# A decoder trunk on one core: attention's output projection in seven block products for its first column pair too, the first heads' sums at attention's end, and the recurrence's functions taken by kind

## The chip, the cores and the metric

The kernel runs on 1 core of a Trainium2 chip. The metric is device time of one execution in microseconds (us). The engines are TensorE (PE, matmuls; its weight loads are PEld), VectorE (DVE), ScalarE (ACT), GpSimd (POOL) and SyncE (SP), which here issues transfers.

## The reference

Two layers over 256 tokens of width 2048, in fp32. Layer 0 mixes with two recurrences (RG-LRU and HGRN2), layer 1 with attention; each is followed by an output projection and an MLP.

```python
# RG-LRU of layer 0
r = sigmoid(x @ w_a + b_a); i = sigmoid(x @ w_i + b_i)
log_a = -8 * r * softplus(-lam)
a = exp(log_a); u = sqrt(-expm1(2 * log_a)) * (i * x)      # then h_t = a_t h_(t-1) + u_t
...
# layer 1
qkv = (h @ w_qkv).reshape(bsz, seq, 3, 16, 128)
...
out = (num / den).reshape(bsz, seq, 2048)                   # three dilated windows merged by softmax
h = h + out @ w_o                                           # w_o: 2048 x 2048
h = h + square(relu(rms_norm(h) @ w1)) @ w2
```

## The kernel before

Every fp32 weight passes TensorE as two parts: `hi`, its rounding to fp32r, made by a cast on ScalarE, and `lo`, the rest, made by a subtraction on VectorE. The activations are split in the same way, in halves of one tile (`bufa`, `bufb`). A product of a 128x512 piece of weight with 128 tokens is three matmuls: hi by hi, hi of the weight with lo of the activation, and lo of the weight with hi of the activation. A weight unit is 1 MB (four pieces of 128x512 rows); for the 256 tokens it takes 24 matmuls. Raw, hi and lo have three buffers each, so units are loaded and split up to three ahead.

**Block products.** Most matrices are taken a column pair (2 x 512 columns) at a time in `blocks`, which computes a 2x2 block product in seven products for eight. Seven products are named `a, t1, t2, c, t3, d, t4`; each takes 12 matmuls. Four of them take sums of weight tiles (`s` and `t`, added on VectorE or by an accumulating transfer from GpSimd's queue), and `t1, t2, t3, c` take sums of activations, which lie in split form in `formx` or `formh`, one part for each of four pairs m. Each of the four pairs stands for two 128-row pieces of the first half of the rows; the rest of the rows goes through plain units `n` of 24 matmuls. The order of the products of a column pair is a row of `ORDERS`.

For w_o, the projection behind attention, the second column pair ran in `blocks` (through `second`), and the first ran plainly in `tokens`: two column blocks n of four units g. Its rows came in the order `PAIRED`, and each unit was split in two halves of 1024 columns. `mixed_forms(m)` made the sums of heads 2m and 2m+1, between w_o's units; only the second pair read them.

**Attention.** w_qkv is taken in `columns`, six blocks of eleven steps, with the values of the last eight heads last. Between steps run the parts of a head from `attend`: `turned` (transposes), `scores` (with the softmax: Exp on ScalarE, normalising of tile `as` by `ll`), `weights` (transposes of `as`, copied to `qk`), `mixed` (the value product, split into `bufb`). The value products of heads 8 to 15 (`mixes`) run at w_o's start: four after its first unit, four after its second, and then `handover` closes attention's pools.

**The recurrence.** `lru_scan` runs on lane e, in ticks between the matmuls of the input projection; `TICKS` says after which half of a unit a lane moves. Letters a and b are the lanes of HGRN2. `lut` keeps ScalarE's functions in program order, and a function of another table brings an ACT_TABLE_LOAD.

A scheduler orders the instructions of each engine from the program and its priorities; within the input projection the order is as written (`InOrder`). Names in the rows drop to the tile: `L261` is the matmul of `mm`, `L264` the transpose, and `L68` every operation of VectorE and ScalarE that goes through the recording helper.

Of the kernel before, what the change touches and what calls it, by code (L numbers as in the profile page):

```python
# [10 lines left out]
F32 = mybir.dt.float32  # L11
# [9 lines left out]
P = 128  # L21
# [20 lines left out]
def trunk_kernel(ctx, tc, head, x, xtok, xback, cols, tab, masks, pos, fin, w_in, w_gate, w_out, w_qkv, w_o, w1, w2, out):  # L42
# [63 lines left out]
    def plan(src, n):  # L106
        units.extend((src, i) for i in range(n))

    order_of = lambda src, i: ORDERS[0 if src is w1 and i not in (0, 64, ) else 2 if src is w2 and i == 120 else 1]

    def plan2(src, i):
        for what, u in order_of(src, i):
# [9 lines left out]
    for layer in range(2):  # L122
        if layer:
            for i in range(0, 48, 8):
                plan2(w_qkv, i)
            plan(w_o, 8)
            plan2(w_o, 8)
        for q in range(4):
            for src in (w1, w2):
                for n in range(0, 4, 2):  # L130
                    plan2(src, layer * 64 + q * 16 + 4 * n)
# [239 lines left out]
            V.scalar_tensor_tensor(r, t, 1.5, r, op0=OP.add, op1=OP.mult)  # L371

    def tokens(src, i0, mov, kgs=(0, 1, 2, 3), by_k=False, behind=(), then=()):
        ks = PAIRED if src is w_o else range(KB)
        ps = [pmm.tile([P, 512], F32, name="p") for _ in range(2)]
        for g in kgs:
            w = unit(src, i0 + g)
            opens, ends = g == kgs[0], g == kgs[-1]
            hi, lo = ([t[:, i * 512:i * 512 + 512] for i in range(4)] for t in (w.hi, w.lo))
            xs = lambda i, j, at=0: mov[:, ks[4 * g + i], at + j * P:at + j * P + P]  # L380
            if by_k:
                for i in range(4):
                    if ends and i == 1:
                        chain.extend(behind)
                    if src is w_in and not ends:
                        parts = [(j, *p) for p in ((0, hi[i]), (S, hi[i]), (0, lo[i])) for j in range(2)]
                    else:
                        parts = [(j, *p) for j in range(2) for p in ((0, hi[i]), (0, lo[i]), (S, hi[i]))]
                        if opens and not i:
                            parts.insert(1, parts.pop(3))  # L390
                    for n, (j, at_, w_) in enumerate(parts):
                        mm(ps[j], xs(i, j, at_), w_, start=opens and not i and at_ == 0 and w_ is hi[0],
                           stop=ends and i == 3 and not any(p[0] == j for p in parts[n + 1:]))
                    if i % 2 and ticks:
                        tick(ticks.pop(0))
            else:
                for j in range(2):
                    if ends and not j:
                        chain.extend(behind)
                    parts = [(i, *p) for i in range(4) for p in ((0, hi[i]), (S, hi[i]))]  # L400
                    parts += [(i, 0, lo[i]) for i in range(4)]
                    for n, (i, at_, w_) in enumerate(parts):
                        mm(ps[j], xs(i, j, at_), w_, start=opens and not n, stop=ends and n == 11)
                    if ticks:
                        tick(ticks.pop(0))
            turn_some(1)
            for f in steps.pop(0) if steps else ():
                f()
            for m in then[kgs.index(g)] if then else ():
                mixed_forms(m)  # L410
        return ps

    def tick(which):
# [281 lines left out]

    def lru_scan(gp):
        gr, gi = rooms[gp][:, :4], rooms[gp][:, 4:]
        for half in range(2):
            for m in range(2 * half, 2 * half + 2):
                b = 4 * gp + m  # L700
                V.tensor_tensor(xc[:, b], xc[:, b], gi[:, m], OP.mult)
                lut(gi[:, m], gr[:, m], AF.Tanh, scale=sp4[:, b:b + 1])
                lut(gr[:, m], gr[:, m], AF.Exp, scale=sp8[:, b:b + 1])
                V.tensor_scalar(gi[:, m], gi[:, m], -1.0, 1e-30, op0=OP.mult, op1=OP.max)
            yield
        for m in range(4):
            lut(gi[:, m], gi[:, m], AF.Sqrt)
        for half in range(2):
            for m in range(2 * half, 2 * half + 2):
                b = 4 * gp + m  # L710
                V.scalar_tensor_tensor(gi[:, m], gr[:, m], 1.0, gi[:, m], op0=OP.add, op1=OP.mult)
                V.tensor_tensor(xc[:, b], xc[:, b], gi[:, m], OP.mult)
                V.tensor_tensor_scan(xc[:, b], gr[:, m], xc[:, b], 0.0, op0=OP.mult, op1=OP.add)
            yield
# [93 lines left out]
                part_forms(forms, k // 2, 1, slice(0, 4), z.rearrange("p i j (one c) -> p one (i j) c", one=1))  # L808
        turns.extend([-half if forms else 0, lambda half=half: work(half)] for half in range(2))

    def mixed_forms(m):
        z = pair.tile([P, 2, 2, P], F32, name="y1", bufs=2)
        b = bufb[:, 2 * m:2 * m + 2].bitcast(F32)
        V.tensor_tensor(z.rearrange("p i j c -> p i (j c)"), b[..., :S], b[..., S:], OP.add)
        a11, a21, a12, a22 = (z[:, i, j] for i in range(2) for j in range(2))
        combos(a22, a11, a21, a12, a11, a21, a12, a22)
        part_forms(formh, m, 1, slice(0, 4), z.rearrange("p i j (one c) -> p one (i j) c", one=1))

    def out_project(src, gname, kgs, behind=()):
        nrm = Norm()  # L820
        whole = any(src is w for w in (w_out, w_o, ))
        for n in range(2 if whole else 4):
            then = () if not whole else ((((), (), (0,), (1,)), ((2,), (3,), (), ())) if src is w_out else
                                         (((), (), (), (0, 1)), ((), (2,), (3,), ())))[n]
            add_res(tokens(src, 4 * n, bufb, kgs, src is w_o and not n, () if n else behind, then), n, nrm)
            to_features(n, gname, formx if n < 2 else None)
        if whole:
            second(0, 2, nrm, 1.0, -1.0, lambda n: to_features(n, gname, None), None, src)
        return nrm


    def blocks(src, i0, n0, mov, forms, events, final):
# [3 lines left out]
                "t1": lambda i: form(3, i), "t2": lambda i: form(0, i), "t3": lambda i: form(1, i),  # L836
                "c": lambda i: form(2, i)}
        alpha, delta, gamma = (pmm.tile([P, 512], F32, name="p") for _ in range(3))
        beta = psc.tile([P, 512], F32, name=("pd" if i0 % 16 else "pt") if src is w_qkv else "po" if n0 else "pd", bufs=1)
        bank = {"a": beta, "t1": alpha, "t2": beta, "c": alpha, "t3": beta, "d": gamma, "t4": beta}  # L840
        sums = {(0, 0): gamma, (0, 1): beta, (1, 0): alpha, (1, 1): delta}
        opened = []
# [102 lines left out]
        blocks(w1, i0, n0, bufa, formx, {"a": hold("y1", A.copy, 2), "t1": hold("y4", V.tensor_copy), "t2": hold("y2", A.copy),  # L945
                                             "t3": u3}, final)

    def second(i0, n0, nrm, r2, r2n, done, gains, src=w2):
        def to_x(bank, j, n, r, last):
            at = slice(n * 512, n * 512 + 512)  # L950
            with urgent():
# [24 lines left out]
        def u3(bank):  # L976
            to_x(bank, 1, n0 + 1, r2n, True)
            done(n0 + 1)

        blocks(src, i0, n0, bufb, formh,  # L980
               {"a": lambda b: to_x(b, 0, n0, r2, False), "t1": lambda b: to_x(b, 1, n0 + 1, r2, False),
                "t2": u2, "t3": u3, **ends},
               lambda n, j, b: to_x(b, j, n0 + n, r2, (n, j) != (1, 1)))
# [37 lines left out]
                second(layer * 64 + q * 16, n, ends, r2, r2n, done, gains if ends and not gname and not n else None)  # L1021
        return fing

    nrm = out_project(w_out, "nmlp0", (2, 3, 0, 1))
    nx1 = Norm()
    mlp(0, nrm, nx1, "nmix1")
    pairs.close()
# [63 lines left out]
    def attend(hd, z):  # L1091
# [12 lines left out]
        def scores():  # L1104
            with urgent():
# [10 lines left out]
                    lut(s[:, sl], s[:, sl], AF.Exp, bias=nm[:, j:j + 1], accum_out=ll[:, j:j + 1])  # L1116
                V.reciprocal(ll, ll)
                for j, sl in enumerate(both_):
                    V.tensor_scalar(s[:, sl], s[:, sl], ll[:, j:j + 1], None, op0=OP.mult)
            made_s[hd] = s  # L1120

        def weights():
# [37 lines left out]
    for g in range(4):  # L1160
        z = columns(8 + 8 * g, "qk", 2, True)
        todo = [steps.pop(0) if steps else [] for _ in range(14)]
        for i in range(4):
            turned, scores, weights, mixed = attend(4 * g + i, z)
            for at_, f in zip(PLACES[i], (turned, scores, weights, mixed)):
                if f is mixed and g > 1:
                    mixes.append(f)
                else:
                    todo[at_].append(f)
        steps[:] = todo  # L1170
    vgroups.append(columns(40, "vg", 1))
    def handover():
        nonlocal pair, formh
        mixers.close()
        pair, formh = open_pairs(1)

    banks = (("po", 1), ("pd", 1), ("pt", 1), ("pl", 2))
    mixes = [lambda f=f, bank=bank: f(*bank) for f, bank in zip(mixes, banks * 2)]
    steps[:] = [sum(steps, []) + mixes[:4], mixes[4:] + [handover]]
    nrm = out_project(w_o, "nmlp1", (0, 1, 2, 3))  # L1180
    fnorm = Norm(False)
    fing = mlp(1, nrm, fnorm, None)
    done = [n for n in range(4) if n != LAST]
# [2 lines left out]
    with urgent():  # L1186
# [21 lines left out]
        for j in range(2):  # L1208
# [38 lines left out]
TICKS = {  # L1247
# [12 lines left out]
PLACE = {step: n for n, step in enumerate(step for step in ORDER.split() if step[0] != "G")}  # L1260
WARM = 10
ONES = 240
PLACES = ((2, 3, 5, 6), (2, 5, 8, 9), (3, 7, 10, 11), (4, 9, 12, 13))
LINE = 64
SCRATCH = 4096
# [1 line left out]
_B = (("t2", 5), ("c", None))  # L1267
_C = (("t3", None), ("d", 1), ("n", 2), ("t4", None), ("n", 3))
ORDERS = (_A + (("n", 6),) + _B + (("n", 7),) + _C, _A + (("n", 7),) + _B + (("n", 6),) + _C,
          _A + (("n", 7),) + _B + (("n", 6), ("t3", None), ("d", 1), ("n", 2), ("n", 3), ("t4", None)))  # L1270
NOSYNC = mybir.DependencyInfo(mybir.DependencyClass.NoSync, mybir.DependencyReason.DATA)


# [90 lines left out]
```

## Time and profile before

| | |
|---|---|
| median of 3 runs | 2113.86 us (2113.79 to 2114.12) |
| profiled execution, its own time | 2114.33 us |
| its span | 2112.6 us |
| granted TensorE clock | 0.999 |
| TensorE busy | 2103.1 us, 9712 instructions |
| VectorE busy | 1791.8 us |
| ScalarE busy | 1317.2 us |
| read from memory | 496.44 MB |

The time is that of the whole execution; the span is from the first to the last profiled instruction. The shares of busy time are means over stages that differ, so what an edit is worth is read from the stage where it lies: w_o begins near 1343.8 us of the span, and the recurrence's scans lie near 170 to 210 us.

### The profile page before, as it was taken

What the parts mean: (1) busy time and instruction counts of PE and PEld (TensorE: products, weight loads), DVE (VectorE), ACT (ScalarE), POOL (GpSimd) and SP (SyncE); (2) the same over time, 40 slices, a digit from 0 to 9 for tenths busy, and PEclk for the clock granted to TensorE, in tenths of its full rate; (3) what the DMA queues carried; (4) which work ended last, traced back from release to release, by engine and by line L of the source; (5) the groups of instructions that cost most, each with busy time, mean ns of one, the idle gap of its engine ahead of it and who ended that gap; (6) DMA issues with size and microseconds to landing.
All of it is one profiled execution on the core that took longest, in us unless ns stands there. A gap on an engine that the chain in (4) does not pass through costs nothing.

```text
span 2112.6 us, 24846 instructions
## 1 busy us (share of the span) xinstructions
PE 2103.1 (100%) x9712; PEld 1751.9 (83%) x9712; DVE 1791.8 (85%) x1742; ACT 1317.2 (62%) x1353; POOL 72.3 (3%) x89
## 2 busy tenths in 40 slices
PE   9999999999999999999999999999999999999998
PEld 8888888888888888888888888888888888888887
DVE  7686979898888888889998888798988988988887
ACT  7576656675566566466665666566755755755764
POOL 0000000000000000000000000000000000000000
PEclk9999999999999999999999999999999999999999
DMA  8544556878787778778777767477787878787884
GB/s 345 182 162 157 174 205 210 275 237 255 236 281 241 248 239 271 251 245 248 260 243 245 213 218 242 168 235 241 237 255 264 250 231 282 244 246 242 277 261 157
DMA packets 70453, 500.15 MB, mean 237 GB/s; under 512 B 7872, under 2 KB 8128, under 8 KB 10560
## 3 DMA queue, kind: packets, MB, share of 16 engines
q1 hardware_dynamic: 58176, 413.29, 50.7%
q0 software_dynamic: 11872, 84.94, 22.1%
q8 instruction: 76, 1.25, 0.2%
q10 hardware_dynamic: 288, 0.34, 0.0%
q14 instruction: 41, 0.34, 0.0%
HBM read 496.44 MB, written 2.10 MB: 236 GB/s over the span
## 4 chain that ended last, share of the span: by engine, by line
PE 98%; DVE 1%; ACT 1%; issue 0%; DVEq 0%; ACTq 0%
PE p L261 62%; PE pd L261 15%; PE po L261 14%; PE pt L261 3%; PE pl L264 2%; PE pl L261 1%; DVE lo L68 0%; ACT hi L68 0%; DVE xall L68 0%; PE po L326 0%; ACT L68 0%; ACT bufb L68 0%; PE po L264 0%; ACT ho L68 0%; DVE st L68 0%
## 5 line engine op out<-in xcount | busy, mean ns | idle before, releaser
L68 ACT CAST hi<-raw 128x2048 fp32r<-128x2048 f32 (+1 forms) x364 | 660.2, 1820 | 515.9 <-PE p L261 293.5
L68 DVE TENSOR_TENSOR lo<-raw,hi 128x2048 fp32r<-128x2048 f32 (+1 forms) x364 | 788.7, 2171 | 139.1 <-ACT hi L68 136.6
L261 PE MATMUL p<-hi,bufa 128*128 128x512 f32 x2000 | 503.0, 393 | 0.0
L261 PEld LDWEIGHTS p<-hi,bufa 128*128 128x128 f32 x2000 | 372.6, 188 | 75.5 <-ACT tk L68 0.2
L261 PE MATMUL p<-hi,bufb 128*128 128x512 f32 x1264 | 318.2, 390 | 0.0
L68 DVE TENSOR_TENSOR lo<-s,hi 128x2048 fp32r<-128x2048 f32 x120 | 274.3, 2286 | 12.4 <-ACT hi L68 10.3
L261 PEld LDWEIGHTS p<-hi,bufb 128*128 128x128 f32 x1264 | 236.2, 188 | 48.6 <-DVE bufb L68 0.2
L261 PE MATMUL p<-lo,bufa 128*128 128x512 f32 x1000 | 269.4, 389 | 0.0
L68 ACT CAST hi<-s 128x2048 fp32r<-128x2048 f32 x120 | 229.4, 1912 | 57.6 <-PE po L261 23.3
L261 PEld LDWEIGHTS p<-lo,bufa 128*128 128x128 f32 x1000 | 187.8, 188 | 39.4
L261 PE MATMUL p<-lo,bufb 128*128 128x512 f32 x632 | 173.0, 389 | 0.0
L261 PEld LDWEIGHTS p<-lo,bufb 128*128 128x128 f32 x632 | 118.7, 188 | 24.7
L68 DVE TENSOR_TENSOR lo<-t,hi 128x2048 fp32r<-128x2048 f32 x40 | 91.4, 2286 | 4.3 <-ACT hi L68 4.3
L68 ACT CAST hi<-t 128x2048 fp32r<-128x2048 f32 x40 | 76.6, 1915 | 28.1 <-PE pd L261 12.3
L68 DVE TENSOR_TENSOR s<-s,raw 128x2048 f32<-128x2048 f32 x40 | 91.3, 2283 | 1.4 <-DMA raw<-in_w_qkv 1.4
L68 DVE TENSOR_TENSOR s<-raw,t 128x2048 f32<-128x2048 f32 x40 | 91.4, 2284 | 0.3 <-DMA raw<-in_w_o 0.3
L68 ACT ACTIVATE y<-y 128x512 f32<-128x512 f32 x112 | 70.5, 630 | 31.8 <-DVE y L68 31.0
L261 PE MATMUL pd<-hi,bufa 128*128 128x512 f32 x352 | 88.2, 393 | 0.0
L261 PE MATMUL p<-hi,formx 128*128 128x512 f32 x352 | 87.6, 391 | 0.0
L68 DVE SCALAR_TENSOR_TENSOR xall<-p,nm,xall 128x512 f32<-128x512 f32 x64 | 47.9, 748 | 43.6 <-PE p L261 43.6
L261 PE MATMUL po<-hi,bufb 128*128 128x512 f32 (+1 forms) x320 | 78.2, 386 | 0.0
L261 PEld LDWEIGHTS p<-hi,formx 128*128 128x128 f32 x352 | 65.6, 188 | 13.4
(309 smaller groups left out, 2568.0 us busy)
## 6 DMA issues: line engine op xcount, KB each, us to landing
raw<-in_w SPq DMA_DIRECT2D x224, 1024.0 KB, 6.9
raw<-in_w_in SPq DMA_DIRECT2D x45, 1024.0 KB, 4.8
raw<-in_w_qkv SPq DMA_DIRECT2D x42, 1024.0 KB, 7.1
t<-in_w SPq DMA_DIRECT2D x32, 1024.0 KB, 7.1
t<-in_w POOLq DMA_DIRECT2D x32, 1024.0 KB, 8.9
s<-in_w POOLq DMA_DIRECT2D x32, 1024.0 KB, 9.3
raw<-in_w_out SPq DMA_DIRECT2D x15, 1024.0 KB, 4.8
raw<-in_w_o SPq DMA_DIRECT2D x15, 1024.0 KB, 4.9
```

The lines of the kernel that those rows point to most:

```text
L68: i = call(*args, **kw)
L261: chain[:] = [after(T.matmul(*args, **kw), chain)]
L264: chain[:] = [after(T.transpose(out_, in_, ident), chain)]
```

## The change

w_o's first column pair goes through `blocks` as well, with a fourth row of `ORDERS` for it. The sums of the first eight heads go to `formx`; they are emitted with attention's last steps (`FORMS`), through one shared scratch place, the spare columns of the tile `qk` of heads 8 to 11. At `handover`, which now comes after the fourth step of w_o, the names formx and formh change places. The eight value products of heads 8 to 15 run after `d` and after the first plain unit. For heads 12 to 15 the normalising is a ScalarE operation. `lru_scan` takes four Tanh, then four Exp, then four Sqrt, with one more place to stop, and two rows of `TICKS` are written anew. w_o's weights are split whole, and `PAIRED` is no longer used in `tokens`.

```diff
-    order_of = lambda src, i: ORDERS[0 if src is w1 and i not in (0, 64, ) else 2 if src is w2 and i == 120 else 1]
+    order_of = lambda src, i: ORDERS[3 if src is w_o and not i else
+                                    0 if src is w1 and i not in (0, 64, ) else 2 if src is w2 and i == 120 else 1]
...
-            plan(w_o, 8)
+            plan2(w_o, 0)
             plan2(w_o, 8)
...
-        ks = PAIRED if src is w_o else range(KB)
+        ks = range(KB)
...
     def lru_scan(gp):
         gr, gi = rooms[gp][:, :4], rooms[gp][:, 4:]
-        for half in range(2):
-            for m in range(2 * half, 2 * half + 2):
-                b = 4 * gp + m
-                V.tensor_tensor(xc[:, b], xc[:, b], gi[:, m], OP.mult)
-                lut(gi[:, m], gr[:, m], AF.Tanh, scale=sp4[:, b:b + 1])
-                lut(gr[:, m], gr[:, m], AF.Exp, scale=sp8[:, b:b + 1])
-                V.tensor_scalar(gi[:, m], gi[:, m], -1.0, 1e-30, op0=OP.mult, op1=OP.max)
-            yield
+        for m in range(4):
+            b = 4 * gp + m
+            V.tensor_tensor(xc[:, b], xc[:, b], gi[:, m], OP.mult)
+            lut(gi[:, m], gr[:, m], AF.Tanh, scale=sp4[:, b:b + 1])
+        yield
+        for m in range(4):
+            lut(gr[:, m], gr[:, m], AF.Exp, scale=sp8[:, 4 * gp + m:4 * gp + m + 1])
+            V.tensor_scalar(gi[:, m], gi[:, m], -1.0, 1e-30, op0=OP.mult, op1=OP.max)
+        yield
         for m in range(4):
             lut(gi[:, m], gi[:, m], AF.Sqrt)
+        yield
...
-    def mixed_forms(m):
-        z = pair.tile([P, 2, 2, P], F32, name="y1", bufs=2)
+    def mixed_forms(m, forms, z=None):
+        if z is None:
+            z = pair.tile([P, 4, P], F32, name="y1", bufs=2)
...
-    def out_project(src, gname, kgs, behind=()):
+    def out_project(src, gname):
         nrm = Norm()
...
+            second(0, 0, nrm, 1.0, -1.0, done, None, src, formx)
+        second(0, 2, nrm, 1.0, -1.0, done, None, src)
         return nrm
...
-        beta = psc.tile([P, 512], F32, name=("pd" if i0 % 16 else "pt") if src is w_qkv else "po" if n0 else "pd", bufs=1)
+        beta = psc.tile([P, 512], F32, name=("pd" if i0 % 16 else "pt") if src is w_qkv else "po" if n0 else "pt" if src is w_o else "pd", bufs=1)
...
                 for j, sl in enumerate(both_):
-                    V.tensor_scalar(s[:, sl], s[:, sl], ll[:, j:j + 1], None, op0=OP.mult)
+                    if hd < 12:
+                        V.tensor_scalar(s[:, sl], s[:, sl], ll[:, j:j + 1], None, op0=OP.mult)
+                    else:
+                        A.activation(s[:, sl], s[:, sl], AF.Copy, scale=ll[:, j:j + 1])
...
+    def head_forms(m):
+        with urgent():
+            mixed_forms(m, formx, held_t[2][:, :, 384:])
+
+    steps.extend([] for _ in range(14 - len(steps)))
+    for m, at_ in enumerate(FORMS):
+        steps[at_].append(lambda m=m: head_forms(m))
     vgroups.append(columns(40, "vg", 1))
     def handover():
-        nonlocal pair, formh
+        nonlocal pair, formh, formx
         mixers.close()
-        pair, formh = open_pairs(1)
-
-    banks = (("po", 1), ("pd", 1), ("pt", 1), ("pl", 2))
+        pair, new = open_pairs(1)
+        formh, formx = formx, new
+
+    banks = (("po", 1), ("pd", 1), ("pl", 2), ("pl", 2))
...
-    steps[:] = [sum(steps, []) + mixes[:4], mixes[4:] + [handover]]
-    nrm = out_project(w_o, "nmlp1", (0, 1, 2, 3))
+    steps[:] = [sum(steps, []), mixes[:4], [], mixes[4:] + [handover]]
+    nrm = out_project(w_o, "nmlp1")
...
-    "f0": "e e . e e . ab .",
+    "f0": "e e e e e . ab .",
...
-    "v1": "ab e ab e ab e ab e",
+    "v1": "ab e ab ee ab e ab e",
...
+FORMS = (6, 8, 9, 10)
...
+          (("a", 0), ("d", 1), ("t1", 4), ("n", 6)) + _B + (("n", 7), ("t3", None), ("n", 2), ("t4", None), ("n", 3)))
```

ScalarE at attention's end, before: `as,ll` is the last head's Exp, `vg` the values, `bufb_83` the activations of heads 8 to 11.

```order
L68 ACTIVATE as,ll<-as,nm 128x128
L68 ACTIVATE as,ll<-as,nm 128x256
L68 ACT_TABLE_LOAD
L68 ACTIVATE spare<-epsc 128x1
L68 CAST hi<-raw 128x1024 x2
L68 ACTIVATE vg<-pd,nr_7933 128x512
L68 COPY qk<-pl 128x384
L68 CAST hi<-raw 128x1024 x2
L68 COPY qk<-pl 128x384
L68 CAST bufb_83<-po 128x256
```

The same place after:

```order
L68 ACTIVATE as,ll<-as,nm 128x128
L68 CAST hi<-s 128x2048
L68 ACTIVATE as,ll<-as,nm 128x256
L68 ACT_TABLE_LOAD
L68 ACTIVATE spare<-epsc 128x1
L68 ACTIVATE vg<-pd,nr_7933 128x512
L68 CAST formx<-qk 128x512
L68 COPY qk<-pl 128x384
L68 CAST hi<-raw 128x2048
L68 ACTIVATE as<-as,ll 128x128
L68 ACTIVATE as<-as,ll 128x256
L68 COPY qk<-pl 128x384
```

The normalising of the last head (`as<-as,ll`) is new on ScalarE, behind two weight casts, the table load, the values, the cast of a sum and a copy.

VectorE at w_o's start, before: `y` is the scratch of a sum of heads, `bufb_81` the first heads.

```order
L68 TENSOR_TENSOR bufb_10091<-pd,bufb_10091 128x256
L68 TENSOR_TENSOR y_10182<-bufb_81 128x512
L68 TENSOR_TENSOR y_10190<-bufb_81 128x512
L68 TENSOR_TENSOR bufb_10091<-pt,bufb_10091 128x256
L68 TENSOR_TENSOR bufb_10091<-pl,bufb_10091 128x256
L68 TENSOR_TENSOR y_10182<-y_10182 128x128
L68 TENSOR_TENSOR y_10190<-y_10190 128x128
```

And after, where `qk` is the shared scratch and `bufb_82` holds heads 4 to 7:

```order
L68 TENSOR_TENSOR qk<-bufb_82 128x4x128
L68 TENSOR_TENSOR lo<-raw,hi 128x2048
L68 TENSOR_TENSOR qk<-qk 128x128 x2
L68 TENSOR_TENSOR bufb_83<-po,bufb_83 128x256
L68 TENSOR_TENSOR qk<-qk 128x128
L68 TENSOR_TENSOR bufb_83<-pd,bufb_83 128x256
L68 TENSOR_TENSOR qk<-qk 128x128
L68 TENSOR_TENSOR bufb_83<-pl,bufb_83 128x256 x2
L68 TENSOR_TENSOR formx<-qk,formx 128x512
L68 TENSOR_TENSOR qk<-bufb_82 128x4x128
L68 TENSOR_TENSOR qk<-qk 128x128 x4
L68 TENSOR_TENSOR formx<-qk,formx 128x512
```

Two sums, which had a scratch each before, follow one another through one scratch, the first between the value products of heads 8 to 11, the second behind them.

ScalarE in the recurrence, in the projection step v1: `bufb_1497` is the scan's room, `sp_364` marks a Tanh, `sp_362` an Exp, `st` a copy of HGRN2. Before:

```order
L68 CAST hi<-raw 128x2048
L68 ACTIVATE bufb_1497<-bufb_1497,sp_364 128x256
L68 ACT_TABLE_LOAD
L68 ACTIVATE bufb_1497<-bufb_1497,sp_362 128x256
L68 ACTIVATE bufb_1497<-bufb_1497,sp_364 128x256
L68 ACTIVATE bufb_1497<-bufb_1497,sp_362 128x256
```

After, where `ho` are the copies of the head sums:

```order
L68 ACTIVATE bufb_1497<-bufb_1497,sp_364 128x256 x4
L68 CAST hi<-raw 128x2048
L68 COPY st<-pl 128x2x128 x2
L68 ACT_TABLE_LOAD
L68 ACTIVATE bufb_1497<-bufb_1497,sp_362 128x256 x4
L68 ACT_TABLE_LOAD
L68 ACTIVATE bufb_1497<-bufb_1497 128x256 x4
L68 CAST hi<-raw 128x2048
L68 ACTIVATE ho,hs<-pd 128x128 x4
```

The kinds stand together, and the Sqrt with its table load comes ahead of the head sums.

More of the change, by code (lines that the diff above doesn't have):

```diff
@@ L409, in tokens @@
             for m in then[kgs.index(g)] if then else ():
-                mixed_forms(m)
+                mixed_forms(m, formh)
         return ps
@@ L809, in to_features @@
         turns.extend([-half if forms else 0, lambda half=half: work(half)] for half in range(2))
-    def mixed_forms(m):
-        z = pair.tile([P, 2, 2, P], F32, name="y1", bufs=2)
-        b = bufb[:, 2 * m:2 * m + 2].bitcast(F32)
-        V.tensor_tensor(z.rearrange("p i j c -> p i (j c)"), b[..., :S], b[..., S:], OP.add)
-        a11, a21, a12, a22 = (z[:, i, j] for i in range(2) for j in range(2))
+    def mixed_forms(m, forms, z=None):
+        if z is None:
+            z = pair.tile([P, 4, P], F32, name="y1", bufs=2)
+        b = bufb[:, 2 * m:2 * m + 2].bitcast(F32).rearrange("p i (h j c) -> p h i j c", h=2, j=2)
+        V.tensor_tensor(z.rearrange("p (i j) c -> p i j c", i=2), b[:, 0], b[:, 1], OP.add)
+        a11, a21, a12, a22 = (z[:, n] for n in range(4))
         combos(a22, a11, a21, a12, a11, a21, a12, a22)
-        part_forms(formh, m, 1, slice(0, 4), z.rearrange("p i j (one c) -> p one (i j) c", one=1))
-    def out_project(src, gname, kgs, behind=()):
+        part_forms(forms, m, 1, slice(0, 4), z[:, None])
+    def out_project(src, gname):
         nrm = Norm()
[L821 to L828, printed above, removed]
+        done = lambda n: to_features(n, gname, formx if n < 2 else None)
+        if src is w_out:
+            for n in range(2):
+                add_res(tokens(src, 4 * n, bufb, (2, 3, 0, 1), then=(((), (), (0,), (1,)), ((2,), (3,), (), ()))[n]), n, nrm)
+                done(n)
+        else:
+            second(0, 0, nrm, 1.0, -1.0, done, None, src, formx)
+        second(0, 2, nrm, 1.0, -1.0, done, None, src)
         return nrm
@@ L946, in first, with second @@
                                              "t3": u3}, final)
-    def second(i0, n0, nrm, r2, r2n, done, gains, src=w2):
+    def second(i0, n0, nrm, r2, r2n, done, gains, src=w2, forms=None):
         def to_x(bank, j, n, r, last):
@@ L978, in u3 @@
             done(n0 + 1)
-        blocks(src, i0, n0, bufb, formh,
+        blocks(src, i0, n0, bufb, formh if forms is None else forms,
                {"a": lambda b: to_x(b, 0, n0, r2, False), "t1": lambda b: to_x(b, 1, n0 + 1, r2, False),
@@ L1022, in mlp @@
         return fing
-    nrm = out_project(w_out, "nmlp0", (2, 3, 0, 1))
+    nrm = out_project(w_out, "nmlp0")
     nx1 = Norm()
@@ L1118, in scores @@
                 for j, sl in enumerate(both_):
-                    V.tensor_scalar(s[:, sl], s[:, sl], ll[:, j:j + 1], None, op0=OP.mult)
+                    if hd < 12:
+                        V.tensor_scalar(s[:, sl], s[:, sl], ll[:, j:j + 1], None, op0=OP.mult)
+                    else:
+                        A.activation(s[:, sl], s[:, sl], AF.Copy, scale=ll[:, j:j + 1])
             made_s[hd] = s
@@ L1269 @@
 ORDERS = (_A + (("n", 6),) + _B + (("n", 7),) + _C, _A + (("n", 7),) + _B + (("n", 6),) + _C,
-          _A + (("n", 7),) + _B + (("n", 6), ("t3", None), ("d", 1), ("n", 2), ("n", 3), ("t4", None)))
+          _A + (("n", 7),) + _B + (("n", 6), ("t3", None), ("d", 1), ("n", 2), ("n", 3), ("t4", None)),
+          (("a", 0), ("d", 1), ("t1", 4), ("n", 6)) + _B + (("n", 7), ("t3", None), ("n", 2), ("t4", None), ("n", 3)))
 NOSYNC = mybir.DependencyInfo(mybir.DependencyClass.NoSync, mybir.DependencyReason.DATA)
```

## The prediction

> **What bounds the kernel now.** I read the page first, then the waits of TensorE, then the chain of work in order of time, and then the timelines around the three places that the change touches.
>
> ```profile
> span 2112.6 us, 24846 instructions
> PE 2103.1 (100%) x9712; PEld 1751.9 (83%) x9712; DVE 1791.8 (85%) x1742; ACT 1317.2 (62%) x1353; POOL 72.3 (3%) x89
> PE 98%; DVE 1%; ACT 1%; issue 0%; DVEq 0%; ACTq 0%
> PE pt L261 <- DVE bufb L68: 0.6, 1, 0.6
> 1425.96 5.44 PE po L261 x24
> ```
>
> TensorE (PE) is busy throughout and is 98% of the chain. Past the start of the program its waits hold one stall of note, the fourth row. The last row prices TensorE's work: 24 matmuls of 128x512 pass in 5.44 us, 0.2267 us each from start to start. So the time falls by what leaves TensorE's queue, and rises by every wait that the other engines put into it. The profiled execution took 2114.33 us with its span of 2112.6; the median shown is 2113.86, so what I add up against the execution goes onto the median.
>
> **Part 1, fewer products.** w_o's first column pair took 8 weight units of 24 matmuls, 192. The new order has seven products of 12 and four plain units of 24, 180. That removes 12 x 0.2267 = **2.72 us**, all on the path.
>
> **Part 2, scans by kind.** This is the only place where TensorE waits now:
>
> ```profile
> 222.18 0.40 PE L261 MATMUL pl<-near,ones_r 128*128 128x256 f32 x2
> 222.79 0.51 PE L261 MATMUL pt<-bufb,ones_r 128*128 128x512 f32 x1 [0.21 <-ACT bufb L68]
> 223.93 0.50 PE L261 MATMUL pt<-bufb,ones_r 128*128 128x512 f32 x1 [0.63 <-DVE bufb L68]
> 224.26 0.40 PE L261 MATMUL pl<-near,ones_r 128*128 128x256 f32 x2
> 203.25 1.28 ACT L68 ACT_TABLE_LOAD   x1
> 205.79 1.90 ACT L68 CAST hi<-raw 128x2048 fp32r<-128x2048 f32 x1
> 207.70 1.28 ACT L68 ACT_TABLE_LOAD   x1
> 209.63 0.88 DVE L68 SCALAR_TENSOR_TENSOR xall<-pd,omlb,xall 128x256 f32<-128x256 f32 x2 [1.53 <-ACT xall L68]
> 218.61 0.68 DVE L68 TENSOR_TENSOR st<-xall 128x512 f32<-128x512 f32 x1
> ```
>
> Two matmuls of 256 columns should pass in 0.23 us from 222.18, but the next starts 0.61 later; then 1.14 and 0.33 pass where one matmul takes 0.227. The excess is 0.38 + 0.91 + 0.10 = 1.39 us. It waits for VectorE's (DVE's) chain, which itself waited 1.53 us at 209.63 for ScalarE (ACT). ScalarE was late because the Sqrt table load and four Sqrt stood at 203.25 to 205.79, between its copies of the head sums and its weight cast. The change puts them ahead of those copies, so these 2.54 us leave that stretch. ScalarE starts it some 0.3 us later, hence VectorE's chain runs about 2.2 us earlier, more than the 1.39. I take **-1.39 us** for this; if VectorE turns out to be bound by its own work between 209.63 and 218.61, it is 0. The number of table loads stays the same.
>
> **Part 3, attention's last heads normalised on ScalarE.** Rows around the end of attention:
>
> ```profile
> 1340.83 1.98 PE L261 MATMUL pd<-hi,bufa 128*128 128x512 f32 x8
> 1341.35 0.49 ACT L68 ACTIVATE as<-as,nm 128x256 f32<-128x256 f32 x1
> 1341.95 1.28 ACT L68 ACT_TABLE_LOAD   x1
> 1342.17 0.55 DVE L68 TENSOR_SCALAR as<-as,ll 128x128 f32<-128x128 f32 x2
> 1343.25 0.20 ACT L68 ACTIVATE spare<-epsc 128x1 f32<-128x1 f32 x1
> 1343.55 0.49 PE L264 MATMUL pl<-tab__184,as 128*128 128x128 f32 x3
> 1345.24 0.68 ACT L68 ACTIVATE vg<-pd,nr 128x512 f32<-128x512 f32 x1
> 1345.82 0.46 ACT L68 COPY qk<-pl 128x384 f32<-128x384 f32 x1
> 1349.38 0.49 PE L264 MATMUL pl<-tab__184,as 128*128 128x128 f32 x3
> L68 ACT CAST hi<-s 128x2048 fp32r<-128x2048 f32 x120 | 229.4, 1912 | 57.6 <-PE po L261 23.3
> 222.12 0.62 ACT L68 CAST bufb<-st 128x512 fp32r<-128x512 f32 x1 [1.13 <-DVE st L68]
> L68 ACT CAST bufb<-po 128x256 fp32r<-128x256 f32 x10 | 3.6, 364 | 0.0
> ```
>
> Before, VectorE scaled the last head's weights at 1342.17 and TensorE turned them only at 1349.38, behind a whole unit: 7 us to spare. Now that unit is half as long: TensorE reaches the transposes at 1343.80 + 2.72 = 1346.52. And the scaling is two operations on ScalarE that stand at the end of this queue: a weight cast (it can start when its buffer's products end, 1340.83 + 1.98 = 1342.81), Exp, table load, spare, vg, the new formx cast, the qk copy, another weight cast. By the rows, start to start: 1.9 + 0.6 (1341.35 to 1341.95) + 1.3 + 0.1 + 0.58 + 0.6 + 0.45 + 1.9 = 7.4 us, so they start near 1350.1 less some overlap (casts that follow one another start 1.8 apart): 1349.9. Two small operations of 0.3 to 0.36 (the last row, the nearest in shape) end by 1350.5, and the transposes follow. Instead of 1346.8 the next product starts at 1350.8: **+4.0 us**. The bounds: 0, if the cast before the Exp finds its buffer and passes earlier, or if these operations overlap more; 5, if every one takes its full busy time and a hand-over. I take 4.0, since each term has a row of its own within ten microseconds. Queued behind the scaling stands the qk copy that the last value product needs; that is inside this wait.
>
> **Part 4, the sums of the first heads before w_o's second product.** They go into formx, through one shared scratch place, so pair 2 must be split before pair 3 can be added. t1 reads all four pairs. VectorE has pair 3's additions behind the low halves of the value products. Rows for a value product and the links behind it:
>
> ```profile
> 1351.67 0.82 PE L261 MATMUL pl<-qk,vg 128*128 128x256 f32 x4
> 1352.24 0.48 PE L261 MATMUL p<-hi,bufb 128*128 128x512 f32 x1
> 1352.68 0.40 ACT L68 CAST bufb<-pl 128x256 fp32r<-128x256 f32 x1
> 1386.94 1.14 DVE L68 TENSOR_TENSOR y<-y 128x128 f32<-128x128 f32 x4
> ```
>
> From t1's turn on TensorE: 0.44 until ScalarE takes the last value product (1352.24 to 1352.68), 0.36 for its cast, 0.62 high half of pair 2, 0.68 low half, 0.68 addition of pair 3, 1.14 its four combinations, 0.62 high half, 0.68 low half: 5.22 us. (The 0.68 is the 128x512 row at 218.61.) t1's eighth matmul is the first that needs pair 3's low half, 7 x 0.2267 + 0.09 = 1.68 us in. So TensorE loses 5.22 - 1.68 = **3.54 us**. The bounds are 0, if pair 2's high half passes ahead of the value products' casts and the four mixes cover more, and 5, if t1 cannot start at all before pair 3.
>
> **Part 5, what is covered.** Eleven weight units instead of eight must be split, with two more additions of whole weights on VectorE, and two as accumulating transfers:
>
> ```profile
> 1344.00:1394.00 50.00, 50.00 (x236) 41.81 (x235) 38.42 (x63) 26.41 (x42) 0.86 (x1) 1.00 0.53 175
> 1296.21 2.29 DVE L68 TENSOR_TENSOR s<-s,raw 128x2048 f32<-128x2048 f32 x1 [0.68 <-DMA raw<-in_w_qkv]
> t<-in_w_o SPq DMA_DIRECT2D x1, 1024.0 KB, 6.0
> s<-in_w_o POOLq DMA_DIRECT2D x1, 1024.0 KB, 10.3
> ```
>
> In those 50 us VectorE works 38.42 and ScalarE 26.41. VectorE gets five operations of 2.29, 11.5 us, and some four additions into the residual, 3 us; two of the four sums of heads (2.5 each by the rows above: 0.68 + 1.14 + 0.68) leave for attention's end, -5. That is 48 us of work in 50 less 2.7 of fewer products, plus the two stalls: just enough, with the weights split up to three units ahead. I cost it at 0, bound 0 to 3 (48 against 47.3, and a backlog where the work bunches). ScalarE gets three casts, 5.7 us, and has room. SP's queue has one more t tile among the raws of w_o, GpSimd's two more transfers. In my walk the first sum is issued near 1365.5 and lands 10.3 later, at 1375.8, for a product near 1380; the t tile of the next block lands near 1383, for a use near 1385. I cost them at 0; a transfer late by 4 us would cost TensorE 2.
>
> **The sum.** -2.72 - 1.39 + 4.0 + 3.54 = +3.43 us on the execution: 2117.76. On the median: 2113.86 + 3.4 = **2117.3 us**. About 0.2%, 4.2 us, is what a measurement of this kernel can tell from no change; 2109.6 to 2118.1 counts as the same.
>
> **Rivals.**
>
> *The gap makes TensorE slow for a while* (slower). At the start of the program the clock shows itself:
>
> ```profile
> 5.42 1.94 PE L261 MATMUL p<-hi,bufa 128*128 128x512 f32 x4
> 7.66 1.09 PE L261 MATMUL p<-hi,bufa 128*128 128x512 f32 x4
> ```
>
> The same four matmuls take 1.94 us at 5.42 and 1.09 at 7.66: TensorE starts at about half rate and keeps it for some 6 us after its first work. If the gap of part 3, 1346.5 to 1350.2, resets it, half of 3 to 6 us is lost, 1.5 to 3. It decides from the length of that one gap: the stalls that the trace has, 0.9 us at most, left no slow stretch. Time 2117.3 + 2.2 = 2119.5. Chance 0.15: one such gap, of a length that the trace has nowhere amid work. [...]
>
> *The waits are hidden* (faster). ScalarE works only 26 of 50 us there, and TensorE never waited for it in this stretch before. If its queue in truth runs ahead of my walk, or the copies beat the second cast, part 3 or part 4 shrinks. One of the two gone: 2113.8 or 2113.3; half of both gone: 2113.5; both gone: 2113.86 - 4.11 = 2109.75, just inside "the same". Against it: the queue's order is fixed, the cast ahead cannot start before a product ends, and without the stalls VectorE's 48 us stand against 47.3. Chance 0.20, of which 0.05 passes the 0.2%.
>
> *The stall at 222 us stays* (the change does not do what the order suggests there). VectorE's chain from 209.63 to 218.61 is long and may be bound by its own scans, which move too. Then 1.39 comes back: 2118.7. Chance 0.10.
>
> **How the numbers follow.** Forecast with both new stalls 0.55, about 2115 to 2118.5; clock 0.15; hidden 0.20; stall stays 0.10. The range leaves out both waits gone (about 0.08) and the upper part of the clock case with part of the second bound (about 0.10): 2111.0 to 2119.8. Slower by over 0.2%: clock 0.15, stall stays 0.10, and 0.05 of the forecast's own upper edge, 0.30. Faster by over 0.2%: 0.05. The same: 0.65.
>
> **What would show it right or wrong.** In the profile after: 12 fewer instructions of PE; no wait of pt for bufb near 222 us; in TensorE's waits a row of pl on ScalarE's as of about 4 us, and one or more of formx on VectorE or ScalarE, 3.5 together, just behind it; 1.00 as the granted clock of that stretch. Slow matmuls of 0.43 spacing behind the gap would show the first rival. It is wrong if the scaling on ScalarE is done before 1346.5, if t1 starts with pair 3 ready, if w_o's later units wait for a DMA, or if the copies of the head sums near 204 us, with ScalarE 0.3 later, now hold TensorE.

## The result and the profile after

| | before | after |
|---|---|---|
| median of 6 runs | 2114.18 us (2113.79 to 2114.41) | 2122.47 us (2120.50 to 2122.67) |
| profiled execution | 2114.33 us | 2120.50 us |
| its span | 2112.6 us | 2118.7 us |
| granted clock of the runs after | | 0.995 to 0.998 |

The ratio after to before is 1.0037, with the interval 1.0027 to 1.0048: 8.3 us slower. The prediction was 2117.3 us in a range of 2111.0 to 2119.8, so it missed on the high side. The profiled execution is the fastest of the six after.

The page's head and TensorE's waits, after (microseconds in total, times, the longest):

```profile
span 2118.7 us, 24834 instructions
PE 2103.9 (99%) x9700; PEld 1750.7 (83%) x9700; DVE 1802.4 (85%) x1735; ACT 1327.2 (63%) x1356; POOL 74.2 (4%) x91
PE pl L265 <- ACT as L68: 3.6, 1, 3.6
PE p L262 <- ACT formx L68: 2.2, 1, 2.2
PE p L262 <- DVE formx L68: 0.2, 1, 0.2
```

Twelve instructions of TensorE are gone, and yet its busy time is 0.8 us more. The wait of pt for bufb is no longer in the list; both foreseen waits are. The timeline at the end of attention, after:

```profile
1342.94 0.51 ACT L68 ACTIVATE as<-as,nm 128x256 f32<-128x256 f32 x1
1343.56 1.28 ACT L68 ACT_TABLE_LOAD   x1
1344.97 0.67 ACT L68 ACTIVATE vg<-pd,nr 128x512 f32<-128x512 f32 x1
1345.54 0.61 ACT L68 CAST formx<-qk 128x512 fp32r<-128x512 f32 x1
1346.42 1.91 ACT L68 CAST hi<-raw 128x2048 fp32r<-128x2048 f32 x1
1348.22 0.81 ACT L68 ACTIVATE as<-as,ll 128x128 f32<-128x128 f32 x2
1348.68 0.83 PE L265 MATMUL pl<-tab__184,as 128*128 128x128 f32 x3 [3.58 <-ACT as L68]
1349.27 2.82 PE L262 MATMUL p<-hi,bufb 128*128 128x512 f32 x8
1351.89 1.91 PE L262 MATMUL p<-lo,bufb 128*128 128x512 f32 x4
1353.60 0.92 PE L262 MATMUL po<-qk,vg 128*128 128x256 f32 x4
```

ScalarE comes to the last head's scaling at 1348.22, behind the Exp, the table load, the values, the sum's cast and a weight cast. TensorE's transposes wait 3.58 us for it. The next product `d` then takes 4.33 us (1349.27 to 1353.60) where 2.72 is its price: its last four matmuls alone take 1.91 us, against 1.07 elsewhere. The windows of the same stretch give the granted clock. Its columns are the length, the busy time (and instructions) of PE, PEld, DVE, ACT and POOL, then the clock, the DMA share and GB/s:

```profile
1338.00:1345.10 7.10, 7.10 (x33) 5.52 (x31) 4.95 (x7) 4.44 (x8) 0.00 (x0) 1.00 1.00 400
1345.10:1348.60 3.50, 0.00 (x0) 0.00 (x0) 3.35 (x5) 3.50 (x6) 0.00 (x0) 1.00 0.27 115
1348.60:1350.30 1.70, 1.55 (x8) 1.18 (x9) 1.70 (x3) 0.91 (x3) 0.00 (x0) 1.00 0.00 0
1350.40:1353.70 3.30, 3.30 (x10) 2.53 (x9) 1.97 (x3) 1.57 (x1) 0.00 (x0) 0.50 0.22 40
1353.90:1360.50 6.60, 4.52 (x22) 3.17 (x20) 4.65 (x12) 2.44 (x7) 0.00 (x0) 1.00 0.32 135
1360.70:1364.00 3.30, 3.12 (x7) 2.20 (x8) 0.69 (x1) 1.69 (x2) 0.00 (x0) 0.50 0.02 5
1364.10:1400.00 35.90, 35.90 (x169) 29.93 (x168) 29.45 (x24) 19.50 (x23) 1.73 (x2) 1.00 0.69 205
```

TensorE idles from 1345.1 to 1348.7 at clock 1.00. Some 1.7 us after it has work again the clock goes to 0.50, and it goes to 0.50 once more at the end of the second wait. Narrower windows put the two stretches at 1350.39 to 1353.80 and 1360.63 to 1364.04, 3.41 us each. The timeline of the second wait:

```profile
1356.79 0.63 ACT L68 CAST formx<-qk 128x512 fp32r<-128x512 f32 x1
1358.17 0.69 DVE L68 TENSOR_TENSOR qk<-bufb 128x512 f32<-128x512 f32 x1
1358.90 1.27 DVE L68 TENSOR_TENSOR qk<-qk 128x128 f32<-128x128 f32 x4
1360.20 0.62 ACT L68 CAST formx<-qk 128x512 fp32r<-128x512 f32 x1 [2.79 <-DVE qk L68]
1360.88 1.52 PE L262 MATMUL p<-hi,formx 128*128 128x512 f32 x2 [2.17 <-ACT formx L68]
1362.19 1.91 PE L262 MATMUL p<-lo,formx 128*128 128x512 f32 x4
1363.90 2.05 PE L262 MATMUL p<-hi,bufb 128*128 128x512 f32 x8
```

Pair 2's split, pair 3's addition, its combinations and its split follow one another through the one scratch, and t1 waits for the last of them. The sum of the profiled execution: -2.7 for the products, -1.4 for the wait at 222 us, +4.1 at the transposes (the product behind them starts at 1349.27 and could have near 1345.2: four matmuls from 1344.02, and 0.25 for the transposes), +1.6 of half clock in `d`, and +4.9 in t1 (1356.24 to 1363.90 is 7.66, less 2.72), of which about 1.1 is half clock in its last five matmuls (0.2 each, and 0.1 in the gaps). Together +6.5; the execution shows +6.2.

### The profile page after: what moved, and what is told of

It reads as the page before. It is cut to its first block, busy times and chain, and to the rows that moved or that the text cites. A ratio compares the mean times of both kernels' runs of the same rounds, so it can differ in the third digit from the quotient of the medians.

```text
span 2118.7 us, 24834 instructions
## 1 busy us (share of the span) xinstructions
PE 2103.9 (99%) x9700; PEld 1750.7 (83%) x9700; DVE 1802.4 (85%) x1735; ACT 1327.2 (63%) x1356; POOL 74.2 (4%) x91
## 4 chain that ended last, share of the span: by engine, by line
PE 99%; ACT 1%; DMA 0%; DVE 0%; SPq 0%; issue 0%; DVEq 0%
PE p L262 62%; PE pd L262 15%; PE po L262 14%; PE pt L262 3%; PE pl L265 2%; PE pl L262 2%; DMA both_in<-in_head 0%; ACT hi L68 0%; PE po L265 0%; DVE qk L68 0%; PE pd L265 0%; PE pt L265 0%; ACT formx L68 0%; SPq L220 0%; DVE xall L68 0%; ACT L68 0%
## 5 line engine op out<-in xcount | busy, mean ns | idle before, releaser
L262 PE MATMUL p<-hi,bufb 128*128 128x512 f32 x1192 | 296.8, 391 | 0.0
L68 DVE TENSOR_TENSOR lo<-s,hi 128x2048 fp32r<-128x2048 f32 x123 | 281.2, 2286 | 14.2 <-ACT hi L68 12.4
L68 ACT CAST hi<-s 128x2048 fp32r<-128x2048 f32 x123 | 235.5, 1915 | 65.3 <-PE pd L262 25.7
L262 PEld LDWEIGHTS p<-hi,bufb 128*128 128x128 f32 x1192 | 223.3, 188 | 46.2 <-DVE bufb L68 0.2
L262 PE MATMUL p<-lo,bufb 128*128 128x512 f32 x596 | 160.3, 391 | 0.0
L262 PEld LDWEIGHTS p<-lo,bufb 128*128 128x128 f32 x596 | 112.4, 189 | 23.5
L262 PE MATMUL p<-hi,formx 128*128 128x512 f32 x384 | 97.3, 394 | 2.5 <-ACT formx L68 2.2
L262 PEld LDWEIGHTS p<-hi,formx 128*128 128x128 f32 x384 | 71.8, 188 | 18.4 <-ACT formx L68 3.0
```

What stands on the lines that cost most here:

```text
L68: i = call(*args, **kw)
L262: chain[:] = [after(T.matmul(*args, **kw), chain)]
```

## The experiments

The theory: two waits at w_o's start, one for the scaling on ScalarE and one for the shared scratch, and a halved clock behind each. Rivals are given with each run.

**Scaling back on VectorE.**

```diff
-                    if hd < 12:
+                    if hd < 16:
```

> The changed kernel with one part undone: the last four heads are normalised on VectorE again. Theory (two waits and the clock that they halve): the wait of about 4.2 us at the last transposes goes, with the half-clock window behind it (1.6 us); the wait of t1 for the sums of heads stays at 3.5 to 4.1 us, with about 1 us of half clock. 2114.2 - 4.1 + 3.5 to 5.1 = 2113.6 to 2115.2 us. Rival (ScalarE's queue is late as a whole, the scaling only shows it): the last value products then wait for the copy of the weights behind the same casts, 3 us or more, and the time stays above 2117.

Measured: 2118.11 us (2117.59 to 2119.47), ratio to before 1.0019 (1.0010 to 1.0028). This is 4.4 us less than the changed kernel, but 3 above what was expected. TensorE's waits in it, and from its timeline the first value products:

```profile
PE p L262 <- ACT formx L68: 3.5, 2, 2.2
PE pl L265 <- DVE as L68: 1.1, 1, 1.1
PE p L262 <- DVE formx L68: 0.6, 2, 0.4
1349.09 0.81 PE L262 MATMUL po<-qk,vg 128*128 128x256 f32 x4
```

The last head's transposes no longer wait, so the scaling's place was that wait's cause, and the last value products do not wait either: the rival's mechanism is not there, though the time did stay above 2117, as it had said. But a new wait of 1.1 us stands at an earlier head's weights, whose scaling is now in VectorE's queue, and t1's wait grew from 2.4 us to 4.1: TensorE comes to the value products 4.5 us sooner (1349.09 for 1353.60), and the chain through the scratch did not come as much sooner. Part of a removed wait was handed on to the next. In its trace the clock is 0.50 from 1358.1 to 1361.5, right behind the last wait for formx; its mean over the execution is 0.998.

**Two scratches.**

```diff
-            mixed_forms(m, formx, held_t[2][:, :, 384:])
+            mixed_forms(m, formx, held_t[2 + m % 2][:, :, 384:])
```

> The changed kernel with a scratch of its own for odd pairs, the spare columns of the next group's tile. Theory: the wait of t1 for the sums goes (4.1 us with its half-clock part); the wait at the last transposes stays, 4.2 to 4.8 us, with 1.6 us of half clock. 2114.2 - 4.1 + 5.8 to 6.4 = 2115.9 to 2116.5 us, up to 2117.5 where the phase of the clock's windows is worse. Rival (t1 waits for VectorE's amount of work, not for the shared scratch): t1 still waits over 2 us, and the time stays above 2118.

Measured: 2117.12 us (2115.80 to 2118.60), ratio 1.0013 (1.0004 to 1.0022); the theory's 2115.9 to 2117.5 holds the median. The waits, and the last split of the sums:

```profile
PE pl L265 <- ACT as L68: 4.7, 2, 3.3
PE p L262 <- ACT hi L68: 0.3, 1, 0.3
1352.32 0.69 DVE L68 TENSOR_TENSOR formx<-qk,formx 128x512 fp32r<-128x512 f32 x1
```

t1 waits for no sum any more: the shared scratch was that wait's cause, not the amount of work. TensorE comes to t1 2.1 us later here (1358.37 for 1356.24), but that does not hide the wait, since the last split ends at 1353.0. ScalarE's scaling now holds TensorE twice, 1.4 and 3.3 us; the 1.4 was not foreseen. At the end of the second the clock is 0.50 for 6.8 us (1349.1 to 1355.9; the eight and four matmuls of `d` take 3.76 and 1.91 us there), where the theory's first figure had one stretch of 1.6 us lost. A phase of the clock's windows, from which the theory had its 2117.5, is shown by no run.

**Both.**

> Both edits together: normalising on VectorE and two scratches. Theory: no wait over 0.5 us is left around w_o's start, the granted clock is 1.0 there, and the gains stand alone: 2114.2 - 2.7 - 1.4 = 2110.1 us, at most 2110.6. Rival (VectorE has too little room in w_o's first pair, 48 us of work against 47): a wait of 1 to 3 us for a low half appears in w_o's first pair, 2111 to 2113.

Measured: 2112.53 us (2112.11 to 2114.01), ratio 0.9994 (0.9984 to 1.0003). Both foreseen waits are gone, but the time is 1.9 us above the theory's upper bound, and inside the rival's 2111 to 2113; the interval of the ratio includes no change. The rows of its waits and of VectorE at the one that is new:

```profile
PE pl L265 <- DVE as L68: 2.3, 1, 2.3
1328.79 2.28 DVE L68 TENSOR_TENSOR s<-raw,t 128x2048 f32<-128x2048 f32 x1
1330.99 0.69 DVE L68 TENSOR_TENSOR qk<-bufb 128x512 f32<-128x512 f32 x1
1331.59 2.29 DVE L68 TENSOR_TENSOR lo<-raw,hi 128x2048 fp32r<-128x2048 f32 x1
1333.79 0.69 DVE L68 TENSOR_TENSOR qk<-bufb 128x512 f32<-128x512 f32 x1
1334.39 0.55 DVE L68 TENSOR_SCALAR as<-as,ll 128x128 f32<-128x128 f32 x2
1334.82 0.61 PE L265 MATMUL pl<-tab__184,as 128*128 128x128 f32 x3 [2.27 <-DVE as L68]
```

Head 13's scaling stands behind the addition of w_o's first weights, a low half and two additions of sums. VectorE's work is what holds TensorE, as in the rival, but the wait did not come in w_o's first pair, where the rival put it; it came at attention's end. The ten times fall into two groups, six at 2112.1 to 2112.6 and four at 2113.7 to 2114.0. The profiled run is of the first group, and its clock is 1.00 from 1322 to 1394; that the second group has a half-clock stretch is inferred from the step of some 1.6 us.

**The scans alone**, on the kernel before: only `lru_scan` and its two rows of `TICKS`.

> The kernel before with only the scans taken by kind and their two rows of ticks. Theory: the wait near 222 us goes and nothing else moves: 2114.2 - 1.4 = 2112.8 us. Rival (ScalarE 0.3 us later at the head sums holds TensorE): 2113.1 to 2114.

Measured: 2112.38 us (2112.23 to 2112.99), ratio 0.9991 (0.9982 to 1.0001): -1.8 us, and no wait near 222 us in its trace. The theory's sign and place hold; the median moved 0.4 more than the wait itself, while the two profiled executions differ by 1.3 (2114.33 to 2112.99). The interval of the ratio just includes no change, so it is the trace that shows the gain.

**Only the last head on VectorE**, with two scratches:

```diff
-                    if hd < 16:
+                    if hd < 12 or hd == 15:
```

> Two scratches, and only the last head normalised on VectorE, heads 12 to 14 on ScalarE as in the changed kernel. Theory: the wait of 2.3 us that both edits left at 1332 us (an earlier head's weights, whose normalising stood behind an addition and a low half of 2.3 us each on VectorE) goes, nothing takes its place: 2114.2 - 2.7 - 1.4 = 2110.1 us, at most 2110.8, clock 0.999 in every run. Rival (these engines have no room there, a wait always appears somewhere): 2111.5 to 2114.

Measured: 2117.16 us (2116.61 to 2117.87), ratio 1.0014 (1.0005 to 1.0023). The theory failed here, and the rival's 2111.5 to 2114 did not hold the time either. The rows at the last head:

```profile
1347.14 0.69 DVE L68 TENSOR_TENSOR formx<-qk,formx 128x512 fp32r<-128x512 f32 x1 [1.61 <-ACT formx L68]
1347.75 2.28 DVE L68 TENSOR_TENSOR s<-s,raw 128x2048 f32<-128x2048 f32 x1
1349.95 0.54 DVE L68 TENSOR_SCALAR as<-as,ll 128x128 f32<-128x128 f32 x2
1350.38 0.61 PE L265 MATMUL pl<-tab__184,as 128*128 128x128 f32 x3 [3.48 <-DVE as L68]
```

The scheduler put a sum's split and a 2.28 us addition of weights ahead of the scaling on VectorE, where the experiment with both edits had it right behind the reciprocal. (An earlier head's scaling on ScalarE holds TensorE for another 1.4 us, and behind the wait of 3.48 us the clock is 0.50 from 1351.7 to 1355.1.) The engine that does the scaling does not decide; what stands ahead of it in that queue does.

**The gaps filled.** Matmuls of no use where TensorE would idle, in the changed kernel:

```diff
+    def fill(n):
+        with urgent():
+            d = psc.tile([P, 512], F32, name="po", bufs=1)
+            for _ in range(n):
+                mm(d, bufb[:, 0, :P], bufb.tiles[0][:, 1], start=True, stop=True, skip_group_check=True)
...
+                if hd == 15:
+                    fill(16)
...
-    steps[:] = [sum(steps, []), mixes[:4], [], mixes[4:] + [handover]]
+    steps[:] = [sum(steps, []), mixes[:4] + [lambda: fill(14)], [], mixes[4:] + [handover]]
```

> The changed kernel with matmuls that compute nothing of use put where TensorE would wait: 16 ahead of the last transposes (3.6 us), 14 ahead of t1 (3.2 us). Theory (the clock halves because TensorE idles): the last heads' weights and the sums come no earlier, so the waits' 4.2 and about 3.5 us stay as work, but no half clock follows: clock 0.999 in all runs, 2117.5 to 2118.8 us, spread under 1 us. Rival (the half clock has another cause, or the lost time beyond the waits is not the clock): 2120.5 or more, with half-clock stretches in the trace.

Measured: 2117.36 us (2116.87 to 2117.44), ratio 1.0014 (1.0005 to 1.0024), 0.1 us below the theory's range; clock 0.999 in all ten runs. The kernel does 30 matmuls more and is 5.1 us faster than the changed one. The product `d` in it:

```profile
1344.97 3.79 PE L262 MATMUL po<-bufb 128*128 128x512 f32 x16
1349.31 2.10 PE L262 MATMUL p<-hi,bufb 128*128 128x512 f32 x8
1351.24 1.08 PE L262 MATMUL p<-lo,bufb 128*128 128x512 f32 x4
```

It starts at 1349.31, as in the changed kernel (1349.27), so the delay was the same; its matmuls take 2.10 and 1.08 us where they took 2.82 and 1.91. So here the half clock came from the idle TensorE: the filled gap is as long, only the idling is gone, and the clock is 1.00 from 1344 to 1394. The time agrees with the sum: 2114.3 - 4.1 + 30 x 0.2267 = 2117.0.

**The first gap filled only.**

> The changed kernel with the 16 matmuls ahead of the last transposes only. Theory: the half clock behind the first gap goes (1.6 us in the profiled run, up to 3.2 where two windows are halved), that behind t1's wait stays (0.8 to 1.6): 2118.9 to 2120.0 us. Rival (the second wait alone is too short to halve the clock, or the first does not cost): as with both filled, or 2122 as before.

Measured: 2118.75 us (2117.17 to 2118.98), ratio 1.0020 (1.0010 to 1.0030), just below the theory's range. Three of the ten runs lie at 2117.2 to 2117.3, seven at 2118.7 to 2119.0. The profiled one is of the three: its trace has the second wait, and the clock in it is 1.00 from 1344 to 1400:

```profile
PE p L262 <- ACT formx L68: 2.4, 1, 2.4
```

So the second wait alone seems to cost about 1.6 us of clock in some executions, and none in others. That the seven have a half-clock stretch is inferred from their step of 1.6 us and from their mean clock, 0.998 in five of them against 0.999 in the three; none of the seven was profiled.

**The sum behind the scaling**, on the kernel with both edits: on VectorE, pair 3's addition is put behind head 13's scaling, and the low halves of pairs 2 and 3 behind head 15's.

```diff
+        if forms is formx and m > 2:
+            after(i, [scaled[13]])
...
-        part_forms(forms, m, 1, slice(0, 4), z[:, None])
+        part_forms(forms, m, 1, slice(0, 4), z[:, None], [scaled[15]] if forms is formx and m > 1 else ())
```

> Both edits of the third experiment, and on VectorE the addition of pair 3 placed behind the normalising of head 13, the low halves of pairs 2 and 3 behind that of head 15. Theory: the one wait left in the third experiment (2.3 us at head 13's transposes) shrinks by the 0.7 us of that addition to 1.6; 2111.4 us, and with a gap that short no run shows a half-clock window: spread under 0.6 us. Rival (that wait is not set by what stands ahead of the scaling on VectorE): 2112.1 or more, with the same two groups of times 1.7 us apart.

Measured: 2111.64 us (2111.15 to 2112.06), ratio 0.9987 (0.9978 to 0.9996). It is 2.7 us below the kernel before, whose median beside it was 2114.38, and below every other version. Its one wait of note besides the start:

```profile
PE pl L265 <- DVE as L68: 1.7, 1, 1.7
```

The wait shrank by 0.6, for 0.7 expected. The eleven times spread over 0.9 us, where under 0.6 was expected, but no second group is seen.

## Why the prediction was wrong

- **Part 1, twelve matmuls, -2.72:** right. TensorE has 12 instructions fewer, and the run that has one wait of 1.7 us left agrees with it (2111.6 is 2114.4 - 4.1 + 1.7, less 0.4).
- **Part 2, the wait at 222 us, -1.39:** right. It is gone after; the scans alone gave -1.3 between profiled executions and -1.8 between medians.
- **Part 3, the transposes, +4.0:** right, with place and links. The wait is 3.58 us by its row, and 4.1 counted at the next product.
- **Part 4, the shared scratch, +3.54:** right in kind and nearly in size: t1 loses 4.9 in the profiled run, about 3.8 without the half clock. The chain ended 5.3 us after t1's turn (1356.24 to 1361.55), for 5.22 foreseen.
- **Part 5, what is covered, 0:** right. No row of TensorE's waits names a weight or a transfer of w_o. But with the scaling back in VectorE's queue (and two scratches) one of the new additions of w_o's weights stood ahead of it, with a low half and two sums, and TensorE waited 2.3 us: the cover holds for this placement only.
- **The clock: this is the step that failed.** It was a rival with a chance of 0.15, decided by the length of one gap of 3.7 us, and was left out of the forecast's sum; its price was 2.2 us, for one gap. That is about the middle of half of 3 to 6 us: the start's rows show the 6, no run shows the 3, and in its place the runs showed stretches of 3.41 and 6.8 us. The second wait was not weighed there at all. The runs show a half clock behind both waits: 2.7 us lost by it in the profiled run (1.6 and 1.1), and more in the others, whose granted clock is down to 0.995. Filling the first gap took 3.7 us off the median, and filling the second as well another 1.4, so the price of 2.2 was too low even for the one gap that it was given to. Without the clock the sum stands: 2114.2 + 3.4 is 2117.6, and the kernel with its gaps filled ran at 2117.4.
- For the median, the clock's part is 2122.5 less some 2117.6, about 5 us. The forecast was thus short of the mechanism that cost the most, and the range ended at 2119.8 because it gave the clock one gap and one price. Which stretches had the half clock in the runs at 2122 was not seen, since only the fastest of them was profiled.

The waits weighed what they were costed at, but the clock behind them was taken too lightly. In the changed kernel it is 0.50 for 3.41 us, twice, the second stretch beginning 10.24 us after the first. The rival had one gap of 3.7 us in view, and a wait as long as that was not needed: in the version with the scaling back on VectorE none of the waits around w_o's start is longer than 2.2 us, and the clock halved half a microsecond behind that one. How short a wait is enough, and what sets the place where a stretch begins, these runs do not show.

The rival's own rows from the start of the program (four matmuls in 1.94 us, later in 1.09) rest on the spacing of the matmuls alone, since the profile's granted clock reads 1.00 there, from 4 to 8 us.

## What to carry to other kernels

When a unit of work on the bound engine gets shorter, look at what the other engines had to have ready by its end: here the same small scaling had 7 us of room before and lacked 4 after. Price a wait of the matmul engine with the half clock that may follow it: here stretches of 3.41 us came with waits of 3.58 and 2.17 us and cost 1.6 and 1.1 us. Weigh every such wait, not only the longest. A gap that cannot be closed may be filled with matmuls of no use, which here cost no more than the wait did and kept the clock at 0.999 in all ten runs. A scratch place shared by two steps makes a chain of them, and a chain is costed link by link from the rows of each link.

## What the runs showed of the hardware that was not expected

- The clock's half stretches did not begin with the gap. In the changed kernel the first began 1.7 us after TensorE had work again, the second 0.25 us before; with two scratches the stretch began 0.6 us before. The first two were 3.41 us long each, and that with two scratches twice as long, 6.8 us.
- The length of a wait alone did not decide whether the clock halved. At the end of a wait of 2.2 us in the changed kernel, and just behind one of 2.2 us with the scaling back on VectorE (where 1.3 and 0.4 stand close ahead), it did; behind one of 2.4 us (the profiled run with the first gap filled) it did not. No half-clock stretch was seen behind a wait of 1.7 us or less that stood alone: with the one of 1.7 the eleven times lie within 0.9 us, and the clock of the profiled run is 1.00 from 1322 to 1394; behind those of 1.4 (two scratches, and the last head only) the next eight matmuls take 2.10 us.
